# A hybrid decoder layer on one core: modulation rows by feature block, scaled rows on ScalarE, a down projection in four column passes

## The chip, the core and the metric

The kernel runs on one core of a Trainium2 chip. Each core has a TensorE for matmuls, VectorE and ScalarE for elementwise work, GpSimd, and SyncE (SP), whose queue issues all transfers of this kernel. The metric is device time in microseconds for one execution; lower is better.

## The reference

One residual layer with two sub-layers, on 256 tokens of 2048 features. A conditioning vector c gives six rows of 2048 numbers: shift, scale and gate for either sub-layer.

```
mod = silu(c) @ w_mod + b_mod                  # 2048 x 12288
sh1, sc1, g1, sh2, sc2, g2 = split(mod, 6)
u = x * (1 + sc1) + sh1
y = token_mixer(u, ...)                        # input projection, mLSTM and HGRN2 heads, w_out
x = layer_norm(ALPHA * x + (1 + g1) * y) * ln1_g + ln1_b
u = x * (1 + sc2) + sh2
y = (silu(u @ w_gate) * (u @ w_up)) @ w_down   # 2048 -> 5632 -> 2048
out = layer_norm(ALPHA * x + (1 + g2) * y) * ln2_g + ln2_b
```

## The kernel before

All weights are float32 and are read once, 512 KB at a time. A weight tile is split into a rounded high part (a copy on ScalarE) and the rest (a subtraction on VectorE); the activations are split in the same way, and every product is three matmuls: high x high, low x high, high x low (`three`, lines 709 to 716). `w1` (line 698 on) issues one tile's transfer on SP's queue into one of 4 raw buffers (`wr`) and makes the two halves, of which 5 each are kept (`wh`, `wl`). The splits have a raised priority.

A modulation row block is 128 output features of `mod`: `mod(j)` (lines 171 to 175) reads 1 MB of transposed `w_mod` into one of two buffers (`mr`) and reduces it on VectorE against silu(c) into column j of `modc`. There are 96: 0 to 15 shift 1, 16 to 31 scale 1, 32 to 47 gate 1, 48 to 63 shift 2, 64 to 79 scale 2, 80 to 95 gate 2. The first 32 belong to the head. Sections 2 and 4 are spread over the rest of the input projection and the output projection: `mods_some(RATE[...])` adds a rate per weight step and takes a row whenever a whole one has come together; `run(modq)` (line 775) takes what is left.

The output projection (lines 749 to 774) runs in four 512-column blocks c, with two PSUM banks for the two token blocks t, its residual (`resid`) and statistics (`stat`) behind each. Then follows the transition to the FFN. Line 776 makes `Ac` = ln1_g x scale and folds ln1_b x scale into the initial value of the rows 48 to 63 (line 778), so that these rows come out as the full bias of u. The rows 48 to 55 (`EARLY`) are taken next. `norm1(t)` normalizes the four blocks of z[t] in place. `make_u2(t, c)` transposes four 128 x 128 blocks of z into a PSUM bank, and for each feature block k makes the scaled row twice: ScalarE writes the high part straight into `u2h`, rounded (line 807), VectorE makes it once more in full (line 809) and subtracts (line 810). For token block 0 and k from 8 on, the row 48 + k is taken inside this loop, and a manual dependence (line 804) holds it behind the first normalizing operation. Token block 1's `make_u2` is written behind all of token block 0's.

The FFN's first two groups run together over 16 steps k with 8 PSUM banks, 24 matmuls of 512 columns a step; the first two steps are done for token block 0 before block 1's rows exist (lines 861 to 874). The groups 2 to 5 follow one at a time; the rows 80 to 95 and the affine of z (lines 884, 885) are written inside them. `down(k0, k1, ...)` runs the down projection over the hidden blocks so far, twice in all (0 to 23, 24 to 43), in two passes e of 1024 columns with four banks. In the very last pass the last two steps k are done for token block 0 first (`skew`), so that its end, `finish(0)`, can overlap with the rest of block 1.

The order on each engine comes from a planner that ranks by program order and raised priority, but starts what is ready early when an engine and a buffer are free in its model. Each engine then runs its own list strictly in that order.

Of the kernel before, what the change touches and what calls it, by code (L numbers as in the profile page):

```python
# [37 lines left out]
EARLY = 8  # L38
# [16 lines left out]
RATE = (0.4, 0.3, 0.4)  # L55
# [24 lines left out]
def build(nc, tc, d):  # L80
    from contextlib import ExitStack

    with ExitStack() as ctx:
# [532 lines left out]
        modq = chain(*[mod_pe(PE_SECT.index(s), s) if s in PE_SECT else chain(*[mod(16 * s + k) for k in range(16)]) for s in (2, 4)])  # L616
# [159 lines left out]
        tt(Ac, pc("l1g", 0, 16), modc[:, 64:80], ALU.mult)  # L776
        tt(Bc, pc("l1b", 0, 16), modc[:, 64:80], ALU.mult)
        tt(init[:, 48:64], init[:, 48:64], Bc, ALU.add)
# [5 lines left out]

        for k in range(EARLY):
            run(mod(48 + k))

        def norm1(t):
            mu, rs = norm(t)
            for c in range(4):  # L790
                w = slice(512 * c, 512 * c + 512)
                i = ts(z[t][:, w], z[t][:, w], mu, rs, ALU.subtract, ALU.mult).ins
                if t == 0 and c == 0:
                    table["first"] = i

        def make_u2(t, c):
            bank = ps()
            for j in range(4):
                nc.tensor.transpose(bank[:, P * j : P * j + P], z[t][:, 512 * c + P * j : 512 * c + P * j + P], ident)
            for j in range(4):  # L800
                k = 4 * c + j
                if t == 0 and k >= EARLY:
                    run(mod(48 + k))
                    tc.add_manual_dep(table["mod"], table["first"].name, order, reason="norm")
                o = bank[:, P * j : P * j + P]
                h = u2(u2h, k, t)
                act(h, o, AF.Identity, scale=Ac[:, k : k + 1], bias=col(3, k))
                u = S(P, "t", bufs=CFG["t"])
                ts(u, o, Ac[:, k : k + 1], col(3, k), ALU.mult, ALU.add)  # L809
                tt(u2(u2l, k, t), u, h.bitcast(F32), ALU.subtract)  # L810
# [44 lines left out]
        use = False  # L855
        for c in range(4):
            make_u2(0, c)
# [8 lines left out]
        for c in range(4):  # L866
            make_u2(1, c)
        for k in range(2):
            block(k, 1)
        for k in range(2, KT):  # L870
            for g in range(2):
                held[k, g] = w1(d["wf"][g * KT + k])
            for t in range(2):
                block(k, t)
        pend = []
# [32 lines left out]
        def down(k0, k1, G, last):  # L908
            for e in range(2):
                bk = [[ps(), ps()] for t in range(2)]  # L910
                held = {}
                skew = 2 if last and e else 0
                for k in range(k0, k1):
                    held[k] = w1(d["wd"][44 * e + k])
# [96 lines left out]
```

## Time and profile before

| | us |
|---|---|
| median of 3 runs | 1316.38 |
| lowest and highest | 1313.13, 1317.86 |
| profiled execution, whole time | 1315.63 |
| its span, first to last instruction | 1313.8 |
| TensorE, VectorE, ScalarE busy | 1222.5, 913.0, 585.3 |

The span is one execution of the kernel under the profiler. A busy share over the whole span mixes stages with different limits; the slices and the windows show where an engine falls short. "Idle before" names what ended an engine's wait.

### The profile page before, as it was taken

How to read it: one execution, taken by the hardware profiler on the slowest of the kernel's cores; microseconds unless marked ns; L12 is line 12 of the kernel's file. 1: busy time of each engine (PE TensorE's matmuls, PEld its weight loads, DVE VectorE, ACT ScalarE, POOL GpSimd, SP SyncE). 2: the span in 40 equal slices, each digit the busy share in tenths (PEclk: the TensorE clock that was granted, in tenths of full speed). 3: DMA queues.
4: the chain of work that ended last, by engine and by line, in shares of the span. 5: the costliest groups of instructions: out<-in, count | busy, mean ns of one | idle time of the engine just before them, and what ended most of it. 6: DMA issues, size and time to landing. Idle time of an engine off the chain costs nothing.

```text
span 1313.8 us, 17232 instructions
## 1 busy us (share of the span) xinstructions
PE 1222.5 (93%) x6738; PEld 1048.4 (80%) x6738; DVE 913.0 (69%) x1026; ACT 585.3 (45%) x728; POOL 3.9 (0%) x13
## 2 busy tenths in 40 slices
PE   4899999899999996289999999999999999999994
PEld 4889999898989885168888888888888888888883
DVE  6789997999998799997845444445455444445555
ACT  4563445545656433234444444433334444434330
POOL 0000000000000000000000000000000000000000
PEclk9999999899999998689999999999999999999997
DMA  9999997667988889689856566566666666676651
GB/s 368 370 339 349 352 404 259 241 225 248 323 304 327 337 325 350 240 307 331 293 189 191 184 196 186 170 193 194 194 192 192 191 184 188 193 253 191 192 162 65
DMA packets 75970, 328.03 MB, mean 250 GB/s; under 512 B 8432, under 2 KB 8816, under 8 KB 62704
## 3 DMA queue, kind: packets, MB, share of 16 engines
q1 hardware_dynamic: 75888, 326.92, 72.0%
q8 instruction: 53, 0.87, 0.3%
q14 instruction: 29, 0.24, 0.0%
HBM read 324.79 MB, written 2.10 MB: 249 GB/s over the span
## 4 chain that ended last, share of the span: by engine, by line
PE 86%; DVE 8%; DMA 2%; issue 2%; ACT 1%; DVEq 0%; SPq 0%; ACTq 0%
PE ps L716 20%; PE ps L713 20%; PE ps L712 20%; PE ps L249 5%; PE ps L251 5%; PE ps L250 5%; DVE m L174 4%; DMA m<-in_wmod 2%; PE ps L260 2%; PE ps L261 2%; PE ps L262 2%; PE ps L445 1%; DVE wl L213 1%; PE ps L835 1%; DVE wl L706 1%
## 5 line engine op out<-in xcount | busy, mean ns | idle before, releaser
L128 ACT ACTIVATE wh<-wr 128x1024 fp32r<-128x1024 f32 x408 | 431.1, 1059 | 569.7 <-PE ps L713 426.9
L706 DVE TENSOR_TENSOR wl<-wr,wh 128x1024 fp32r<-128x1024 f32 x296 | 361.5, 1225 | 327.5 <-ACT wh L128 326.9
L712 PE MATMUL ps<-wh,u2h 128*128 128x512 f32 x704 | 277.2, 394 | 10.1 <-DVE t L809 9.8
L713 PE MATMUL ps<-wh,u2l 128*128 128x512 f32 x704 | 276.0, 393 | 2.0 <-DVE u2l L810 2.0
L174 DVE CUSTOM_DVE_ANT_0 m<-m,cb,init 128x2048 f32<-128x2048 f32 x96 | 225.1, 2346 | 10.5 <-DMA m<-in_wmod 10.1
L716 PE MATMUL ps<-wl,u2h 128*128 128x512 f32 x704 | 220.4, 393 | 2.5 <-DVE wl L706 2.4
L249 PE MATMUL ps<-uh,wh 128*128 128x256 f32 x640 | 185.1, 294 | 22.3 <-ACT wh L128 16.7
L250 PE MATMUL ps<-ul,wh 128*128 128x256 f32 x640 | 181.6, 286 | 0.0
L251 PE MATMUL ps<-uh,wl 128*128 128x256 f32 x640 | 180.3, 287 | 1.1 <-DVE wl L213 1.0
L712 PEld LDWEIGHTS ps<-wh,u2h 128*128 128x128 f32 x704 | 133.6, 190 | 39.0 <-DVE t L809 10.7
L716 PEld LDWEIGHTS ps<-wl,u2h 128*128 128x128 f32 x704 | 133.3, 190 | 31.3 <-DVE wl L706 3.3
L713 PEld LDWEIGHTS ps<-wh,u2l 128*128 128x128 f32 x704 | 133.6, 190 | 30.1 <-DVE u2l L810 2.4
L213 DVE TENSOR_TENSOR wl<-wr,wh 128x1024 fp32r<-128x1024 f32 x112 | 135.8, 1221 | 27.0 <-ACT wh L128 26.4
L249 PEld LDWEIGHTS ps<-uh,wh 128*128 128x128 f32 x640 | 124.2, 196 | 24.9 <-ACT wh L128 17.1
L712 PE MATMUL ps<-wh,hid 128*128 128x512 f32 x352 | 137.2, 390 | 0.0
L713 PE MATMUL ps<-wh,hid 128*128 128x512 f32 x352 | 137.0, 389 | 0.0
L250 PEld LDWEIGHTS ps<-ul,wh 128*128 128x128 f32 x640 | 124.7, 195 | 1.2 <-issue 1.0
L251 PEld LDWEIGHTS ps<-uh,wl 128*128 128x128 f32 x640 | 123.2, 194 | 1.9 <-DVE wl L213 1.8
L716 PE MATMUL ps<-wl,hid 128*128 128x512 f32 x352 | 108.4, 389 | 0.0
L713 PEld LDWEIGHTS ps<-wh,hid 128*128 128x128 f32 x352 | 66.1, 188 | 13.7
L716 PEld LDWEIGHTS ps<-wl,hid 128*128 128x128 f32 x352 | 66.1, 188 | 13.7
L712 PEld LDWEIGHTS ps<-wh,hid 128*128 128x128 f32 x352 | 66.1, 188 | 13.6
(177 smaller groups left out, 1031.2 us busy)
## 6 DMA issues: line engine op xcount, KB each, us to landing
m<-in_wmod SPq DMA_DIRECT2D x96, 1024.0 KB, 6.5
wr<-in_wf SPq DMA_DIRECT2D x176, 512.0 KB, 3.6
wr<-in_win SPq DMA_DIRECT2D x112, 512.0 KB, 5.9
wr<-in_wd SPq DMA_DIRECT2D x88, 512.0 KB, 3.6
wr<-in_wo SPq DMA_DIRECT2D x32, 512.0 KB, 5.0
xT<-in_x SPq DMA_DIRECT2D x4, 512.0 KB, 7.7
z<-in_xr SPq DMA_DIRECT2D x2, 1024.0 KB, 7.3
out<-z SPq DMA_DIRECT2D x8, 256.0 KB, 2.4
```

The lines of the kernel that those rows point to most:

```text
L128: i = nc.scalar.activation(out, in_, f, **kw).ins
L174: table["mod"] = nc.vector.tensor_tensor_reduce(t, t, cb, 1.0, init[:, j : j + 1], ALU.mult, ALU.add, modc[:, j : j + 1]).ins
L213: tt(l[:, :m], r[:, :m], h[:, :m].bitcast(F32), ALU.subtract)
L249: mm(o, h[:, wsl], kt(uh, k0 + k), start=st, stop=False, skip_group_check=True)
L250: mm(o, h[:, wsl], kt(ul, k0 + k), start=False, stop=False, skip_group_check=True)
L251: mm(o, l[:, wsl], kt(uh, k0 + k), start=False, stop=en, skip_group_check=True)
L260: mm(o, a, h[:, w], start=first and k == 0, stop=False, skip_group_check=True)
L261: mm(o, a, l[:, w], start=False, stop=False, skip_group_check=True)
L706: tt(l, r, h.bitcast(F32), ALU.subtract)
L712: mm(o, a, h[:, w], start=first, stop=False, skip_group_check=True)
L713: mm(o, b, h[:, w], start=False, stop=False, skip_group_check=True)
L716: mm(o, a, l[:, w], start=False, stop=last, skip_group_check=True)
```

## The change

Sections 3 and 4 (shift 2, scale 2) are ordered by feature block: after the 16 gate rows come the pairs 64 + k, 48 + k. The first 34 rows of this list are spread by raised rates up to the end of the output projection; the other 14, for k = 9 to 15, are taken two at a time in the k loop of the FFN's first two groups from k = 2 on. `Ac` and `Bc` are made per 512-column block c (`affine1`), with Bc = ln1_b x scale + shift as a column of its own. The scaled rows of c = 0 and 1 are made at once for both token blocks, those of c = 2 and 3 at k = 4 and k = 8; their transposes are copied from PSUM into two tiles `zt` by ScalarE meanwhile. A scaled row is made once, by ScalarE, in full; the high part is a copy of four rows at once on ScalarE and the low part one subtraction on VectorE. The manual dependence is gone. The down projection runs in four passes of 512 columns with two banks, a weight tile holding two steps k of 512 columns; the skew of the last pass is 8 steps k.

```diff
--- before.py
+++ after.py
@@ -35,7 +35,7 @@
 
 STAGES = stages(("fq qk g i v", 4), ("qk g i v", 8), ("fq qk g i v", 16), ("o", 16))
 LAG = 0
-EARLY = 8
+FIRST = 34
 MIX = (("qk g i", "first"), ("v", "second"), ("o", "p last n"))
 NATIVE = ((), ())
 PRI = dict(w=400, e=0, m=-200)
@@ -52,7 +52,7 @@
 
 PE_SECT = ()
 DVE_SECT = ()
-RATE = (0.4, 0.3, 0.4)
+RATE = (0.45, 0.4, 0.5)
 CFG = dict(big=10, med=10, wr=4, mr=2, wh=5, wl=5, s5=4, t=3, cm=2)
 
 
@@ -613,7 +613,8 @@
         from itertools import chain
 
         gt["x"] = 0
-        modq = chain(*[mod_pe(PE_SECT.index(s), s) if s in PE_SECT else chain(*[mod(16 * s + k) for k in range(16)]) for s in (2, 4)])
+        order2 = list(range(32, 48)) + [j + k for k in range(KT) for j in (64, 48)]
+        modq = (None for j in order2[:FIRST] for _ in mod(j))
         credit = [0.0]
 
         def mods_some(a):
@@ -773,41 +774,60 @@
                         resid(t, c, banks[c][t], G1, ALPHA)
                         stat(t, c)
         run(modq)
-        tt(Ac, pc("l1g", 0, 16), modc[:, 64:80], ALU.mult)
-        tt(Bc, pc("l1b", 0, 16), modc[:, 64:80], ALU.mult)
-        tt(init[:, 48:64], init[:, 48:64], Bc, ALU.add)
+        late = order2[FIRST:]
+
+        def some(n):
+            for _ in range(n):
+                if late:
+                    run(mod(late.pop(0)))
+
+        def affine1(c):
+            w = slice(4 * c, 4 * c + 4)
+            tt(Ac[:, w], pc("l1g", 4 * c, 4), modc[:, 64 + 4 * c : 68 + 4 * c], ALU.mult)
+            tt(Bc[:, w], pc("l1b", 4 * c, 4), modc[:, 64 + 4 * c : 68 + 4 * c], ALU.mult)
+            tt(Bc[:, w], Bc[:, w], modc[:, 48 + 4 * c : 52 + 4 * c], ALU.add)
+
+        affine1(0)
+        affine1(1)
         u2h = [M(name="u2h", dt=F32R) for _ in range(4)]
         u2l = [M(name="u2l", dt=F32R) for _ in range(4)]
 
         def u2(tiles, k, t):
             return tiles[k // 4][:, (k % 4) * T + t * P : (k % 4) * T + t * P + P]
-
-        for k in range(EARLY):
-            run(mod(48 + k))
 
         def norm1(t):
             mu, rs = norm(t)
             for c in range(4):
                 w = slice(512 * c, 512 * c + 512)
-                i = ts(z[t][:, w], z[t][:, w], mu, rs, ALU.subtract, ALU.mult).ins
-                if t == 0 and c == 0:
-                    table["first"] = i
-
-        def make_u2(t, c):
+                ts(z[t][:, w], z[t][:, w], mu, rs, ALU.subtract, ALU.mult)
+
+        zt = {}
+
+        def turn(t, c):
             bank = ps()
             for j in range(4):
                 nc.tensor.transpose(bank[:, P * j : P * j + P], z[t][:, 512 * c + P * j : 512 * c + P * j + P], ident)
+            if c < 2:
+                zt[t, c] = bank
+                return
+            if t == 0:
+                zt[c] = M(name="zt")
+            zt[t, c] = zt[c][:, 512 * t : 512 * t + 512]
+            act(zt[t, c], bank, AF.Copy)
+
+        def make_u2(t, c):
+            u = S(512, "s5", bufs=CFG["s5"])
             for j in range(4):
                 k = 4 * c + j
-                if t == 0 and k >= EARLY:
-                    run(mod(48 + k))
-                    tc.add_manual_dep(table["mod"], table["first"].name, order, reason="norm")
-                o = bank[:, P * j : P * j + P]
-                h = u2(u2h, k, t)
-                act(h, o, AF.Identity, scale=Ac[:, k : k + 1], bias=col(3, k))
-                u = S(P, "t", bufs=CFG["t"])
-                ts(u, o, Ac[:, k : k + 1], col(3, k), ALU.mult, ALU.add)
-                tt(u2(u2l, k, t), u, h.bitcast(F32), ALU.subtract)
+                w = slice(P * j, P * j + P)
+                act(u[:, w], zt[t, c][:, w], AF.Identity, scale=Ac[:, k : k + 1], bias=Bc[:, k : k + 1])
+
+            def part(x):
+                return x[c].rearrange("p (k t) -> p k t", t=T)[:, :, t * P : t * P + P]
+
+            u3 = u.rearrange("p (k t) -> p k t", t=P)
+            act(part(u2h), u3, AF.Copy)
+            tt(part(u2l), u3, part(u2h).bitcast(F32), ALU.subtract)
 
 
         NG = DFF // 512
@@ -852,9 +872,10 @@
             return bk, held, block
 
         norm1(0)
-        use = False
         for c in range(4):
-            make_u2(0, c)
+            turn(0, c)
+            if c < 2:
+                make_u2(0, c)
         norm1(1)
         use_set(AF.Silu)
         tc.add_manual_dep(table["load"], table["var"].name, order, reason="table")
@@ -864,7 +885,9 @@
                 held[k, g] = w1(d["wf"][g * KT + k])
             block(k, 0)
         for c in range(4):
-            make_u2(1, c)
+            turn(1, c)
+            if c < 2:
+                make_u2(1, c)
         for k in range(2):
             block(k, 1)
         for k in range(2, KT):
@@ -872,6 +895,13 @@
                 held[k, g] = w1(d["wf"][g * KT + k])
             for t in range(2):
                 block(k, t)
+            some(2)
+            for c in (2, 3):
+                if k == 4 * c - 4:
+                    some(max(0, len(late) - 8 * (3 - c)))
+                    affine1(c)
+                    make_u2(0, c)
+                    make_u2(1, c)
         pend = []
         for g in range(2):
             for t in range(2):
@@ -906,27 +936,32 @@
                 pend.append(g)
 
         def down(k0, k1, G, last):
-            for e in range(2):
-                bk = [[ps(), ps()] for t in range(2)]
+            for c in range(4):
+                bk = [ps(), ps()]
                 held = {}
-                skew = 2 if last and e else 0
-                for k in range(k0, k1):
-                    held[k] = w1(d["wd"][44 * e + k])
+                skew = 8 if last and c == 3 else 0
+
+                def pair(k, t):
+                    for j in range(2):
+                        w = slice(512 * j, 512 * j + 512)
+                        three([bk[t]], held[k][0][:, w], held[k][1][:, w], hslice(k + j, t, 0), hslice(k + j, t, 1), k + j == k0, k + j == k1 - 1)
+
+                for k in range(k0, k1, 2):
+                    held[k] = w1(d["wd"][22 * c + k // 2])
                     if k < k1 - skew:
                         for t in range(2):
-                            three(bk[t], *held[k], hslice(k, t, 0), hslice(k, t, 1), k == k0, k == k1 - 1)
-                    if k == k0 + 2:
+                            pair(k, t)
+                    if k == k0 + 4:
                         while pend:
                             flip(pend.pop(0))
                 for t in range(2):
-                    for k in range(k1 - skew, k1):
-                        three(bk[t], *held[k], hslice(k, t, 0), hslice(k, t, 1), False, k == k1 - 1)
-                    for i in range(2):
-                        resid(t, 2 * e + i, bk[t][i], G, None)
-                        if last:
-                            stat(t, 2 * e + i)
-                    if last and e:
-                        finish(t)
+                    for k in range(k1 - skew, k1, 2):
+                        pair(k, t)
+                    resid(t, c, bk[t], G, None)
+                    if last:
+                        stat(t, c)
+                        if c == 3:
+                            finish(t)
 
         def finish(t):
             mu, rs = norm(t)
@@ -973,7 +1008,7 @@
     a["wg"] = tile(np.concatenate([wi[:, 3072:3076], z, wi[:, 3076:3080]], axis=1), 0, KT, 0, 36)
     a["wo"] = np.stack([tile(wo, 8 * part + 2 * p, 2, 512 * i, 512) for part in (1, 0) for i in range(4) for p in range(4)])
     a["wf"] = np.stack([np.concatenate([tile(wg, k, 1, 512 * g, 512), tile(wu, k, 1, 512 * g, 512)], axis=1) for g in range(DFF // 512) for k in range(KT)])
-    a["wd"] = np.stack([tile(wd, k, 1, 1024 * e, 1024) for e in range(2) for k in range(FB)])
+    a["wd"] = np.stack([tile(wd, k, 2, 512 * c, 512) for c in range(4) for k in range(0, FB, 2)])
     a["xr"] = x[0].reshape(2, P, D)
     for n, v in (("l1g", ln1_g), ("l1b", ln1_b), ("l2g", ln2_g), ("l2b", ln2_b)):
         a[n] = v.reshape(1, D)
```

## Rows read from the trace of the kernel before

**Rows 1.** The page: busy time of TensorE with its share of the span, and its busy tenths in 40 equal slices of the span (32.8 us each).

```profile
PE 1222.5 (93%) x6738; PEld 1048.4 (80%) x6738; DVE 913.0 (69%) x1026; ACT 585.3 (45%) x728; POOL 3.9 (0%) x13
...
PE   4899999899999996289999999999999999999994
```

**Rows 2.** Busy time by stretch. Columns: the stretch in us and its length; PE, PEld, DVE, ACT and POOL busy us with the number of instructions; mean granted TensorE clock; DMA share; GB/s.

```profile
164.00:197.00 33.00, 33.00 (x278) 33.00 (x277) 30.39 (x28) 16.29 (x20) 0.00 (x0) 1.00 1.01 405
230.00:263.00 33.00, 28.45 (x352) 27.50 (x353) 32.41 (x45) 19.44 (x32) 0.00 (x0) 0.90 0.68 240
430.00:506.00 76.00, 76.00 (x337) 62.74 (x335) 65.38 (x72) 32.06 (x34) 0.00 (x0) 1.00 0.89 332
506.00:586.00 80.00, 37.72 (x136) 28.84 (x136) 78.27 (x132) 22.26 (x43) 0.00 (x0) 0.70 0.79 289
586.00:645.00 59.00, 59.00 (x261) 48.84 (x261) 47.17 (x45) 26.16 (x25) 0.00 (x0) 1.00 0.90 331
```

**Rows 3.** The waits between 506 and 586 us: engine, line, whom it waited for, us in total, times, longest.

```profile
PE ps L799 <- DVE t L809: 18.1, 2, 13.7
ACT u2h L128 <- DVE modc L174: 10.7, 4, 3.7
...
PE ps L712 <- DVE t L809: 9.8, 2, 6.1
```

**Rows 4.** Groups of VectorE between 506 and 586 us: line, engine, operation, out<-in, shapes, count; busy us, mean ns of one; idle before.

```profile
L174 DVE CUSTOM_DVE_ANT_0 m<-m,cb,init 128x2048 f32<-128x2048 f32 x17 | 39.9, 2345 | 1.2 <-DMA m<-in_wmod 1.2
L809 DVE TENSOR_SCALAR t<-ps,sc,modc 128x128 f32<-128x128 f32 x32 | 12.4, 404 | 0.0
L706 DVE TENSOR_TENSOR wl<-wr,wh 128x1024 fp32r<-128x1024 f32 x8 | 9.5, 1220 | 0.0
L810 DVE TENSOR_TENSOR u2l<-t,u2h 128x128 fp32r<-128x128 f32 x31 | 8.3, 283 | 0.0
L884 DVE SCALAR_TENSOR_TENSOR z<-z,bc 128x512 f32<-128x512 f32 x6 | 4.1, 682 | 0.0
...
L792 DVE TENSOR_SCALAR z<-z,mv 128x512 f32<-128x512 f32 x8 | 4.1, 540 | 0.5 <-ACT mv L128 0.5
```

**Rows 5.** VectorE in order of time, the modulation: start us, us, engine, line, operation, out<-in, shapes, count.

```profile
440.28 0.17 DVE L776 TENSOR_TENSOR sc<-pk,modc 128x16 f32<-128x16 f32 x1
...
502.20 2.34 DVE L174 CUSTOM_DVE_ANT_0 m<-m,cb,init 128x2048 f32<-128x2048 f32 x1
...
511.41 2.34 DVE L174 CUSTOM_DVE_ANT_0 m<-m,cb,init 128x2048 f32<-128x2048 f32 x1
...
546.92 2.34 DVE L174 CUSTOM_DVE_ANT_0 m<-m,cb,init 128x2048 f32<-128x2048 f32 x1
...
551.05 2.35 DVE L174 CUSTOM_DVE_ANT_0 m<-m,cb,init 128x2048 f32<-128x2048 f32 x1
```

**Rows 6.** TensorE in order of time around the hole: start us, us, engine, line, operation, out<-in, shapes, count, and in brackets the idle time before with what ended it.

```profile
505.11 0.39 PE L716 MATMUL ps<-wl,yh 128*128 128x512 f32 x1
...
505.79 0.39 PE L716 MATMUL ps<-wl,yh 128*128 128x512 f32 x1
515.77 3.68 PE L799 MATMUL ps<-kc,z 128*128 128x128 f32 x16 [9.59 <-DVE z L792]
519.10 1.43 PE L712 MATMUL ps<-wh,u2h 128*128 128x512 f32 x4
...
585.74 0.96 PE L716 MATMUL ps<-wl,u2h 128*128 128x512 f32 x3 [2.45 <-DVE wl L706]
```

**Rows 7.** Groups of TensorE between 506.1 and 585.7 us, the matmuls of the FFN (columns as in rows 4).

```profile
L712 PE MATMUL ps<-wh,u2h 128*128 128x512 f32 x35 | 16.1, 473 | 10.1 <-DVE t L809 9.8 <-ACT wh L128 0.3
L713 PE MATMUL ps<-wh,u2l 128*128 128x512 f32 x35 | 15.6, 457 | 2.0 <-DVE u2l L810 2.0
L716 PE MATMUL ps<-wl,u2h 128*128 128x512 f32 x32 | 12.9, 469 | 0.0
```

**Rows 8.** Groups of the whole span by form: VectorE's subtraction over 512 columns (line 231), ScalarE's scaled row and its rounding copy of 512 columns; and a pair of scaled rows on ScalarE in order of time.

```profile
L128 ACT ACTIVATE u2h<-ps,modc,sc 128x128 fp32r<-128x128 f32 x32 | 14.2, 456 | 38.7 <-DVE t L809 22.6 <-DVE modc L174 10.7 <-PE ps L799 5.4
...
L231 DVE TENSOR_TENSOR hid<-ps,hid 128x512 fp32r<-128x512 f32 x22 | 14.0, 682 | 0.0
...
L128 ACT ACTIVATE hid<-ps 128x512 fp32r<-128x512 f32 x22 | 11.6, 586 | 0.0
...
519.72 0.81 ACT L128 ACTIVATE u2h<-ps,modc,sc 128x128 fp32r<-128x128 f32 x2 [2.33 <-DVE t L809]
```

**Rows 9.** VectorE in order of time, the last weight splits ahead of the norm.

```profile
504.47 4.63 DVE L706 TENSOR_TENSOR wl<-wr,wh 128x1024 fp32r<-128x1024 f32 x4
```

**Rows 10.** The end in order of time: VectorE's first residual of the last block, the last matmuls, VectorE's last scaling.

```profile
1291.85 1.29 DVE L723 TENSOR_TENSOR s<-ps,bc 128x512 f32<-128x512 f32 x2 [8.79 <-PE ps L716]
...
1294.14 0.61 PE L716 MATMUL ps<-wl,hid 128*128 128x512 f32 x2
...
1308.85 1.41 DVE L936 SCALAR_TENSOR_TENSOR z<-z,mv,bc 128x512 f32<-128x512 f32 x2
```

**Rows 11.** Transfers of the modulation rows: issues from 586 to 660 us with KB each and median us to landing; the queue of SP in order of time; the reductions between 586 and 645 us.

```profile
m<-in_wmod SPq DMA_DIRECT2D x6, 1024.0 KB, 7.9
...
519.38 49.00 SPq L173 DMA_DIRECT2D m<-in_wmod  x13
...
L174 DVE CUSTOM_DVE_ANT_0 m<-m,cb,init 128x2048 f32<-128x2048 f32 x8 | 18.8, 2350 | 6.1 <-DMA m<-in_wmod 6.1
```

## The prediction, made blind

> **What bounds the kernel now.** First the page's busy shares and its 40 slices [rows 1]: TensorE is busy 93% of the span, and only three places fall short of nines: the first two slices, slices 16 to 18, and the last one. The head isn't touched by the change, so the middle and the end are what it can move. Then the windows [rows 2]: from 430 to 506 us and from 586 to 645 us TensorE is busy throughout; from 506 to 586 it is busy 37.7 of 80 us, at a mean granted clock of 0.70, while VectorE is busy 78.3 of the 80 and ScalarE 22.3. VectorE is therefore the bound of that hole. The waits of TensorE there [rows 3] name it too: the transposes of line 799 wait 18.1 us for line 809, the scaled row made on VectorE, and matmuls wait 9.8 us for the same line. ScalarE waits 10.7 us for columns of the modulation (modc).
>
> What VectorE does there [rows 4]: 17 modulation reductions of 2.35 us, 39.9 us in all; 32 pairs of lines 809 and 810, 20.7 us; the rest is weight splitting, the affine and the norm. The order in time [rows 5] explains the hole. Program order makes all of token block 0's scaled rows, which need every shift row 48 to 63, before any of block 1's, and the k loop needs both blocks. The reductions from 511.41 to 546.92 us are these rows; those from 551.05 on are rows of section 5, which run ahead of their place while block 1's scaled rows wait their turn. That running ahead is seen elsewhere as well: the scales' product (line 776), written behind the whole output projection, ran at 440.28 us. So the rates in RATE set a floor to the pace of the rows, not the pace itself.
>
> How large the loss is: the last matmul of the output projection starts at 505.79 us, steady work begins at 585.74 us [rows 6]. Three matmuls take 0.68 us (505.11 to 505.79), 0.227 each, and 102 FFN matmuls were done in between [rows 7], worth 23.1 us. The stretch from 506.0 to 585.7 us, 79.7 us, thus loses 56.6 us.
>
> **The change part by part.**
> *The transition.* The first pair of FFN groups has 16 steps of 24 matmuls, 384 x 0.227 = 87.1 us. Before, 282 of them were left at 585.7 us, so the pair ends at 585.7 + 64.0 = 649.7 us. After the change:
> - Feature blocks 0 and 1 (k = 0 to 7) of both token blocks need only rows 64 to 71 and 48 to 55, all within the first 34. The 14 rows left over no longer stand before any matmul of k = 0 to 7, which are 8 x 5.44 = 43.5 us of TensorE work.
> - The norm's chain stays. I keep 506.0 to 519.1 us [rows 6] for the gap. Now four scaled rows are finished together: ScalarE's four at 0.36 to 0.46 us [rows 8], a rounding copy of 512 columns and a VectorE subtraction of 512 columns, at 0.59 and 0.68 us by the nearest forms [rows 8]. From the first transposes at 515.77 us that is about 0.6 for a first four at the low clock, then 1.6 + 0.6 + 0.7, some 519.7 us for the first complete operands. Before, the matmuls started at 519.1 and waited 2 us more for the low half.
> - After that gap the matmuls run at the lower of the two clock levels for a while: the windows from 506 us average 0.70 [rows 2]. Until about 526 us at half speed, 6.3 us of time, costs 3.2 us. Block 1's 16 transposes, (519.1 - 515.8) / 16 = 0.21 us each at the low clock and half of that at the full one, cost 1.7 us inside the stream.
> - VectorE is relieved: per four rows it had 4 x (0.404 + 0.283) = 2.75 us [rows 4] and now has 0.68, over 8 fours 22.0 down to 5.5 us. ScalarE, idle in 58 of the 80 us [rows 2], takes up 8 copies and 4 copies of transposes, 7 us: hidden. The nine small products of affine1 come to under 2 us; they are hidden in the same way, and would cost that much if VectorE is full.
>
> Undisturbed, the pair ends at 519.7 + 87.1 + 3.2 + 1.7 = 611.7 us, 38.0 us earlier.
>
> *What is late next.* c = 2 needs 6 of the 14 rows at about 519.7 + 4.9 + 43.5 = 568 us, c = 3 needs all at about 590 us. VectorE's work from 509 us, when the last four splits before the norm end [rows 9], to 590 us: 14 rows at 2.35 = 32.9; 19 weight splits at 1.22 = 23.2; the norm's scaling 8 x 0.54 = 4.3; subtractions 5.5; residuals and statistics left over, five operations of about 0.68 and two aggregations, 3.9; a dozen affines at 0.68 = 8.2 [rows 4]. That is 78.0 of 81 us, 96%. The nearest row for such a load is the stretch from 230 to 263 us [rows 2], VectorE 32.4 of 33 us and TensorE idle for 4.55 us of it. Two and a half such stretches would lose 11 us; with the splits given priority over the rows nothing need be lost. I take 8 us, bounds 0 and 28 (the transfers, below). Bytes: 14 rows of 1.05 MB, 17 weight tiles of 0.52 MB and a broadcast of 1.05 MB are 24.6 MB in 82 us, 300 GB/s, under the 332 GB/s at which 430 to 506 us ran with TensorE full [rows 2]. The transition gains 38.0 - 8 = 30.0 us.
>
> *The queues that the rows are moved past.* SP issues rows and weight tiles in one order, and a row waits there for one of two buffers; behind it wait the weight tiles of the next steps, then ScalarE's copies, VectorE's splits and TensorE. On ScalarE the scaled rows of c = 2 and 3 wait for modc, with weight copies queued behind them. Both are priced as rivals.
>
> *Rows earlier.* From 0.4, 0.3, 0.4 to 0.45, 0.4, 0.5 a row: the largest effect is where VectorE is full, about 24 steps x 0.05 = 1.2 rows of 2.35 us in the stretch that begins at 230 us. Cost between 0 and 2.8 us; I take 1, as TensorE falls short in only one window there. By 506 us 71 of the 96 reductions had started, the last at 502.20 [rows 5]; less the 32 of sections 0 and 1 that is 39, so asking for 34 is no extra load in sum.
>
> *Down projection.* The matmuls are the same in number, size and weight loads, the tiles the same 512 KB: nothing. Its end [rows 10]: VectorE works without a break from 1291.85 to 1310.26 us, 15.5 us past TensorE's last matmul (1294.14 + 0.61). It holds the residuals of two column blocks for both token blocks, 12 operations at 0.6, then the final scaling. After the change the residuals of c = 2 run beside the last pass, 6 x 0.6 = 3.6 us less; the skew of 8 instead of 2 double-width steps lets block 0 end 24 instead of 12 matmuls before block 1, 2.7 us sooner; against that the two short waits for the variance on ScalarE have less to fill them, 0.5 to 1.3 us. Gain 5.0 to 5.8, I take 5.3 us. The last transfer behind it stays.
>
> **Sum.** 30.0 - 1 + 5.3 = 34.3 us off the profiled execution's 1315.6 us is 1281.3 us; against the median of 1316.4 us, 1282.1 us. The profiled run lies 0.75 us under the median, which is less than any bound here. I predict 1282 us.
>
> One rule of the skill speaks against a part of this. The Trainium skill, ScalarE: Activation LUTs, section Rules for kernel authors, says to do multiplications and additions on VectorE and not on ScalarE. Here a 128-column scaling takes 0.456 us on ScalarE against 0.404 on VectorE [rows 4, 8], so the rule holds for one operation; but VectorE is the full engine of the hole and ScalarE the empty one, and by the rule alone the change would have to lose 8 x 4 x 0.05 = 1.7 us where the sum sees a gain of 16.5 us of VectorE time.
>
> **The rivals.**
> *The transfers set the pace.* If all 14 rows are still to come when the k loop reaches k = 2, each of the seven steps from 2 to 8 asks for two rows and two tiles, 3.15 MB. At 332 GB/s that is 9.5 us against 5.44 of matmuls: 28 us lost in place of 8, so 1302 us. For it: the issue order in the text is just that. Against it: rows run ahead, and four or five fit into the gap before 519 us.
> The Trainium skill, Perfetto Trace Analysis, section Roofline, gives about 435 GB/s as the ceiling of a single core; at that rate a step would take 7.2 us and the loss would be 13 us. The best stretch here, 164 to 197 us, moved 405 GB/s [rows 2].
>
> *Rows done early, the norm's way free.* If nearly all rows run ahead and the two reductions at 502.20 and 511.41 us no longer stand before the last statistics, there is no stall and the gap shrinks by two rows: 8 + 4.7 us more, 1269 us.
>
> *The hole moves.* Stalls eat the whole transition and only the end gains: 1310 us or so. For that the seven steps would have to take 5.44 + 38 / 7 = 10.9 us each.
>
> *In lockstep, slower.* The row's issue waits for a reduction, the reduction stands behind splits, these wait for buffers that TensorE frees, and the next weights stand behind the row on SP. Then a step is a chain: 5.44 of matmuls, 7.9 us for a row to land [rows 11] and two reductions, 18 us. Seven steps lose 88 us, less 38 and 4.3: 1316 + 46 = 1362 us. It turns slower from a step of about 11.5 us on. Against it: beside the FFN from 586 to 645 us, eight reductions passed the same queues and TensorE missed nothing [rows 2], and from 519 us 13 rows were issued in 49 us [rows 11], 3.8 us each.
> The Trainium skill, TensorE: Matmul & The Clock Gate, section Part 1, calls ScalarE and VectorE strict FIFOs; that is what such a lockstep needs, and the order in time of the rows above is in keeping with it.
>
> **How the numbers follow.** Forecast with stalls of 0 to 16 us (1274 to 1290): 0.60. Transfers (1290 to 1304): 0.20. Early rows (1267 to 1274): 0.10. The hole moves (1304 to 1316): 0.06. Lockstep: 0.04. The range takes in the forecast, the early rows and most of the transfers: 1268 to 1302 us. About 0.5% or 6.6 us is what a measurement of this kernel can tell from no change; below 1309.8 us lie the first three and part of the fourth: faster 0.92, same 0.04, slower 0.04.
>
> **What would show it.** Right: TensorE idle some 13 us from 506 us and then busy with few gaps; lines 809 and 810 gone from VectorE; reductions of rows 57 to 79 between the splits of k = 2 to 8; VectorE's end some 10 us after the last matmul. Wrong: TensorE waiting at k = 5 to 8 for weight tiles, or at k = 8 and 12 for scaled rows, the norm later than 514 us, or a new gap in the stretch that begins at 230 us.

## The result, and the profile after

| | before | after |
|---|---|---|
| median, us | 1317.12 (1313.13 to 1318.16, 4 runs) | 1268.04 (1264.93 to 1270.38, 4 runs) |
| profiled execution, us | 1315.63 | 1270.38 |
| its span, us | 1313.8 | 1268.6 |

The ratio is 0.9631, 95% interval 0.9602 to 0.9661: 49 us between the medians, 45.2 us between the two profiled executions. The forecast was 1282 us; the measured time is that of its rival "rows done early, the norm's way free" (1269). It lies 0.04 us above the lower end of the stated range (1268 to 1302) and outside the stretch that had most of the chance (1274 to 1290). One of five further executions of the unaltered change took 1682.1 us at a mean granted clock of 0.685; the ratios leave it out.

The page, against [rows 1]. In place of the three weak slices in the middle there is one 8:

```profile
PE 1216.6 (96%) x6738; PEld 1045.5 (82%) x6738; DVE 900.4 (71%) x979; ACT 588.6 (46%) x740; POOL 3.9 (0%) x13
...
PE   4899999899999999899999999999999999999995
```

Busy time by stretch, against [rows 2] (columns as there; the stretch from 506 us is cut in two). From 520 to 645 us TensorE misses nothing; before, it was busy for 33.3 of the 66 us from 520 to 586. The stretch that begins at 230 us is as it was:

```profile
230.00:263.00 33.00, 28.56 (x351) 27.48 (x350) 32.20 (x47) 19.78 (x32) 0.00 (x0) 0.90 0.65 231
...
506.00:520.00 14.00, 7.68 (x33) 6.41 (x32) 14.00 (x22) 7.00 (x15) 0.00 (x0) 0.80 0.99 389
520.00:586.00 66.00, 66.00 (x295) 54.02 (x294) 59.55 (x69) 39.60 (x62) 0.00 (x0) 0.99 0.84 302
586.00:645.00 59.00, 59.00 (x270) 49.09 (x269) 50.34 (x49) 27.10 (x30) 0.00 (x0) 1.00 0.93 340
```

VectorE's groups between 506 and 586 us, against [rows 4]. The two lines of scaled rows are gone, 5.5 us of subtractions are left, and 24 weight splits stand where there were 8:

```profile
L707 DVE TENSOR_TENSOR wl<-wr,wh 128x1024 fp32r<-128x1024 f32 x24 | 28.4, 1218 | 2.0 <-ACT wh L128 2.0
L174 DVE CUSTOM_DVE_ANT_0 m<-m,cb,init 128x2048 f32<-128x2048 f32 x11 | 25.7, 2345 | 3.6 <-DMA m<-in_wmod 3.6
L830 DVE TENSOR_TENSOR u2l<-s,u2h 128x512 fp32r<-128x512 f32 x8 | 5.5, 686 | 0.9 <-ACT u2h L128 0.9
```

VectorE in order of time: three modulation reductions, the lines between them left out. The one at 505.23 is the 72nd of 96 (71 start before 499 us). Less the 32 of the head that is 40 done before the norm, where the text asked for 34. Of the rows of shift 2 and scale 2 all for c = 0, 1 and 2 are then there; the eight for c = 3 follow from 517.31 to 563.52:

```profile
505.23 2.34 DVE L174 CUSTOM_DVE_ANT_0 m<-m,cb,init 128x2048 f32<-128x2048 f32 x1
...
517.31 2.34 DVE L174 CUSTOM_DVE_ANT_0 m<-m,cb,init 128x2048 f32<-128x2048 f32 x1
...
563.52 2.34 DVE L174 CUSTOM_DVE_ANT_0 m<-m,cb,init 128x2048 f32<-128x2048 f32 x1
```

TensorE in order of time, against [rows 6]. The wait before the transposes fell from 9.59 to 6.32 us, but the output projection ended 3.4 us later in this execution, so that the transposes start where they did. In four more profiles of kernels with the same program up to there (the unaltered change again, the scaled rows on both engines, the old down projection, the skew of 2) the projection's last matmul starts between 505.50 and 507.71 us and the wait is 6.31 to 6.36 us. The shorter wait thus belongs to the change; the later end varies from profile to profile, and its cause is not shown. The first four matmuls take 2.00 us, the lower clock level, the next pairs 0.62:

```profile
509.19 0.39 PE L717 MATMUL ps<-wl,yh 128*128 128x512 f32 x1
515.89 3.67 PE L809 MATMUL ps<-kc,z 128*128 128x128 f32 x16 [6.32 <-DVE z L802]
519.47 2.00 PE L713 MATMUL ps<-wh,u2h 128*128 128x512 f32 x4
521.30 0.62 PE L714 MATMUL ps<-wh,u2l 128*128 128x512 f32 x2
```

The end, against [rows 10]: token block 0's last residual, TensorE's last matmul, VectorE's last operation. From the end of the one (1254.86) to the end of the other (1265.11) it is 10.2 us, before 15.5:

```profile
1249.46 0.69 DVE L724 TENSOR_TENSOR s<-ps,bc 128x512 f32<-128x512 f32 x1 [6.07 <-PE ps L717]
...
1254.47 0.39 PE L717 MATMUL ps<-wl,hid 128*128 128x512 f32 x1
...
1263.70 1.41 DVE L971 SCALAR_TENSOR_TENSOR z<-z,mv,bc 128x512 f32<-128x512 f32 x2
```

The last Silu products of the first pair of FFN groups, first before, then after, start 39.9 us earlier:

```profile
652.15 1.28 DVE L825 TENSOR_TENSOR s<-s,ps 128x512 f32<-128x512 f32 x2
612.27 1.28 DVE L845 TENSOR_TENSOR s<-s,ps 128x512 f32<-128x512 f32 x2
```

With 5.3 us at the end this is the whole difference of the spans. Everything was gained at the two places that the prediction named, and nothing in between; the 3.4 us by which the projection ended later are already taken off.

### The profile page after: what moved, and what is told of

It is laid out like the page before. It is cut to its first block, busy times and chain, and to the rows that moved or that the text cites. A ratio compares the mean times of both kernels' runs of the same rounds, so it can differ in the third digit from the quotient of the medians.

```text
span 1268.6 us, 17191 instructions
## 1 busy us (share of the span) xinstructions
PE 1216.6 (96%) x6738; PEld 1045.5 (82%) x6738; DVE 900.4 (71%) x979; ACT 588.6 (46%) x740; POOL 3.9 (0%) x13
## 4 chain that ended last, share of the span: by engine, by line
PE 89%; DVE 6%; ACT 2%; issue 2%; DMA 1%; DVEq 0%; ACTq 0%
PE ps L713 21%; PE ps L714 21%; PE ps L717 21%; PE ps L249 5%; PE ps L251 5%; PE ps L250 5%; DVE m L174 2%; PE ps L260 2%; PE ps L261 2%; PE ps L262 2%; PE ps L445 1%; DVE wl L213 1%; ACT wh L128 1%; PE ps L855 1%; DMA m<-in_wmod 1%
## 5 line engine op out<-in xcount | busy, mean ns | idle before, releaser
L717 PE MATMUL ps<-wl,u2h 128*128 128x512 f32 x704 | 217.2, 389 | 0.0
L717 PE MATMUL ps<-wl,hid 128*128 128x512 f32 x352 | 137.0, 389 | 0.0
L714 PEld LDWEIGHTS ps<-wh,hid 128*128 128x128 f32 x352 | 66.1, 188 | 13.5
```

What stands on the lines that cost most here:

```text
L714: mm(o, b, h[:, w], start=False, stop=False, skip_group_check=True)
L717: mm(o, a, l[:, w], start=False, stop=last, skip_group_check=True)
```

## The experiments

The theory to begin with: the order by feature block makes the gain in the middle, VectorE's relief comes second, the end gives some 5 us. The rival: VectorE's relief makes it, in whatever order. The expectations name their own theories A and B, run by run.

**The scaled rows on both engines again, in the new order.** The edit, with the lines of the loop left out:

```diff
-                act(u[:, w], zt[t, c][:, w], AF.Identity, scale=..., bias=...)
-            act(part(u2h), u3, AF.Copy)
-            tt(part(u2l), u3, part(u2h).bitcast(F32), ALU.subtract)
+                act(h, o, AF.Identity, scale=..., bias=...)
+                ts(u, o, Ac[:, k : k + 1], Bc[:, k : k + 1], ALU.mult, ALU.add)
+                tt(u2(u2l, k, t), u, h.bitcast(F32), ALU.subtract)
```

> The changed kernel, but each scaled row made twice again, rounded on ScalarE and in full on VectorE with a subtraction for each 128 columns; the new order of rows stays. Theory A (what closed the hole is the order: the scaled rows of feature blocks 0 and 1 no longer stand behind the last shift rows): VectorE gets 16 us more work but the reductions were done some 20 us before they were needed, so at most a few us: 1268 to 1274. Theory B (what closed it is the relief of VectorE, which was busy 78 of 80 us): the 16.5 us are back on the path, 1280 to 1286.

Measured 1277.21 us, ratio 0.9707 (0.9688 to 0.9726): 9 us of the gain are lost, a fifth. Windows of this kernel (columns as above): VectorE is full from 520 to 540 us, and TensorE misses 3.8 us there, 1.1 us in the next window and 1.9 us from 600 to 620 us, 6.8 us of the 9:

```profile
520.00:540.00 20.00, 16.22 (x72) 11.55 (x71) 20.00 (x33) 11.41 (x24) 0.00 (x0) 1.00 0.74 273
540.00:560.00 20.00, 18.88 (x81) 14.68 (x80) 17.75 (x36) 7.14 (x9) 0.00 (x0) 1.00 0.93 336
...
600.00:620.00 20.00, 18.08 (x78) 14.29 (x78) 17.94 (x20) 9.48 (x11) 0.00 (x0) 1.00 0.92 319
```

In the new order VectorE's relief is worth 9 us. The rule quoted in the prediction from the Trainium skill (ScalarE: Activation LUTs, Rules for kernel authors: multiplications and additions belong on VectorE) gives the wrong sign here for the move as a whole, which also turns 32 subtractions of 128 columns into 8 of 512.

**The old order, the scaled rows on ScalarE.**

```diff
-order2 = list(range(32, 48)) + [j + k for k in range(KT) for j in (64, 48)]
+order2 = list(range(32, 48)) + list(range(64, 80)) + list(range(48, 64))
```

together with the old places of `make_u2` and of the shift rows, and the manual dependence. These go together; no run takes them apart.

> The changed kernel, but with the old order of modulation rows and of scaled rows: sections 2 and 4 first, then the rows 48 to 63, all four blocks c of token block 0 before those of token block 1, the rows from 56 on held behind the first normalization; the scaled rows stay on ScalarE. Theory A: the hole is back, less the work taken from VectorE: 1268 + 38 - 14, some 1292 (1284 to 1302). Theory B: nearly nothing is lost, 1268 to 1276.

Measured 1296.16 us, 0.9852 (0.9833 to 0.9871): the order is worth 28 us. Waits from 506 to 600 us (us in total, times, longest). Besides 6.6 us for the norm, one wait of TensorE stands out, for ScalarE's rows, and ScalarE waits for the bias columns of the later blocks (sc, line 788), which are made from the shift rows:

```profile
PE ps L713 <- ACT u2h L128: 22.7, 1, 22.7
...
ACT s L128 <- DVE sc L788: 16.1, 2, 14.0
```

**The old rates.** `RATE` is 0.4, 0.3, 0.4 again.

> The changed kernel with the old rates 0.4, 0.3, 0.4 and still 34 rows before the transition. In the changed kernel the output projection ends 3.4 us later than before, yet the normalization starts at the same 515.2 us, since VectorE's list sets it. Theory A (hidden there): TensorE ends the projection about 3 us earlier and then waits 3 us longer: 1266 to 1270, no measurable difference. Theory B (the higher rates cost TensorE time that is lost for good): 3.4 us faster, 1264 to 1265.

Measured 1270.74 us, 0.9661 (0.9643 to 0.968). The output projection ends 2.7 us earlier than in the second profile of the unaltered change (its last matmul at 505.03 and 507.71 us), but hardly earlier than in two other profiles with the new rates (505.50 and 505.65), so that this is not shown to come from the rates. The wait for the norm is 1.8 us longer (8.13 and 6.31), and the time is 2 us above the unaltered change, with intervals that just overlap. The higher rates cost nothing that can be measured.

**The old down projection.** `down` with two passes of 1024 columns and the skew of 2, and its weight layout.

> The changed kernel with the old down projection: two passes of 1024 columns, the last two steps skewed. Theory A: only the end changes, VectorE's work behind the last matmul goes from 10.3 back to 15.5 us: 5.2 us slower, 1273. Theory B (the four passes also change the stream of matmuls or the weights' buffers): another number, and TensorE's busy windows before the end differ.

Measured 1273.4 us, 0.9682 (0.966 to 0.9705), 5 us slower; 15.5 us from the end of the last matmul (1250.67) to VectorE's end (1266.17):

```profile
1250.05 0.62 PE L717 MATMUL ps<-wl,hid 128*128 128x512 f32 x2
...
1264.76 1.41 DVE L966 SCALAR_TENSOR_TENSOR z<-z,mv,bc 128x512 f32<-128x512 f32 x2
```

**The change unaltered, once more.** It ran in one set with the next three kernels.

> The changed kernel once more, unaltered. Its first profile ended the output projection 3.4 us later than the kernel before, while two kernels with the same program up to there (the old down projection, the scaled rows on both engines) did not. Theory A (a stall of that one execution): the projection ends at about 506 us and the transposes start at about 512.4 us; median 1265 to 1268. Theory B (a cost of the higher rates): 509 us again.

Measured 1268.62 us, 0.9628 (0.9612 to 0.9645). The projection's last matmul starts at 507.71 us and the transposes at 514.41, between the two theories: neither a stall of a single execution nor a fixed cost of the rates is shown.

**All 14 late rows held behind the norm.** The edit, without the lines that remember the first normalizing operation:

```diff
                     run(mod(late.pop(0)))
+                    tc.add_manual_dep(table["mod"], table["first"].name, order, reason="norm")
```

> The changed kernel with the 14 late modulation rows held behind the first normalizing operation; in the changed kernel 6 of them ran ahead of it. Theory A (the gap before the FFN is VectorE's list: what stands ahead of the norm there delays it): the reduction that ran at 505.23 us is gone from it and the four splits stand partly behind, 2 to 4 us faster, 1262 to 1265, as the 24 us by which the rows were early pay for the later start. Theory B (the late rows had no reserve): TensorE waits at k = 8 and 12, 1270 or more.

Measured 1278.85 us, 0.9712 (0.9694 to 0.9729): 10 us slower, though TensorE waits only 2.7 us in all for the normalized blocks. SP's queue in order of time (start, us until the last of the group was issued, count): two rows, one weight tile, two rows, one weight tile, 9 us a turn. The rows' issues wait for buffers that reductions free, and the tiles stand behind them:

```profile
548.28 3.80 SPq L173 DMA_DIRECT2D m<-in_wmod  x2
552.17 0.38 SPq L702 DMA_DIRECT2D wr<-in_wf  x1
557.60 3.20 SPq L173 DMA_DIRECT2D m<-in_wmod  x2
560.90 0.38 SPq L702 DMA_DIRECT2D wr<-in_wf  x1
566.55 3.80 SPq L173 DMA_DIRECT2D m<-in_wmod  x2
```

The waits from 540 to 580 us: ScalarE waits 29.1 us for weight tiles, and TensorE 7.8 us for ScalarE. The third line is from SP's own waits from 495 to 590 us, the rows' issues waiting for reductions:

```profile
ACT wh L128 <- DMA wr<-in_wf: 29.1, 8, 8.0
...
PE ps L713 <- ACT wh L128: 7.8, 2, 5.1
...
SPq L173 <- DVE modc L174: 45.1, 12, 6.0
```

This has the queue of the prediction's rival "the transfers set the pace", but not its price. A turn of 9 us holds two rows and one tile, where the rival gave two rows and two tiles 9.5 us, and 10 us are lost in all, where it gave 28. The issue that waits for a reduction is the link of the lockstep rival, at half its step of 18 us. Whether the bytes (301 GB/s from 548.28 to 566.55 us) or that chain sets the 9 us, no run separates. With the head start of six rows, none of it showed.

**The norm's chain first.** Raised priority for the residuals and statistics of the output projection's last block and for `norm1(0)`.

```diff
+                        with tc.high_priority(1000 if c == 3 else 0):
                             resid(t, c, banks[c][t], G1, ALPHA)
                             stat(t, c)
...
+        with tc.high_priority(1000):
             norm1(0)
```

> The changed kernel with a raised priority for the last block's residuals and statistics of the output projection and for the first normalization, above that of the weight splits. Theory A (VectorE's list sets the gap): two of the four splits stand behind the norm, 2.3 us faster, 1264 to 1266. Theory B (the chain from the last matmul through the variance sets it): no change, 1266 to 1269.

Measured 1265.19 us, 0.9608 (0.9591 to 0.9625), 3.4 us under the unaltered change, with intervals that overlap a little. In order of time (columns as before, all engines): one reduction still stands before token block 0's last statistics, the aggregate comes at 508.36 us in place of 514.44, and the wait is 3.31 us in place of 6.32:

```profile
503.16 2.35 DVE L174 CUSTOM_DVE_ANT_0 m<-m,cb,init 128x2048 f32<-128x2048 f32 x1
...
508.36 0.25 DVE L735 BATCH_NORM_AGGREGATE mv<-st 128x2 f32<-128x24 f32 x1
...
510.80 3.60 PE L810 MATMUL ps<-kc,z 128*128 128x128 f32 x16 [3.31 <-DVE z L803]
```

**Both together.** The hold of all 14 rows and the raised priority.

> Both edits: late rows held behind the first normalization, and the raised priority of the last residuals and the norm. Theory A: the idle time ahead of the first transposes falls from 6.3 us to 2 us or less; 4 to 5 us faster than the changed kernel, 1262 to 1264. Theory B: as the changed kernel or slower.

Measured 1277.77 us, 0.97 (0.9685 to 0.9715): TensorE waits 0.8 us in all for the normalized blocks, but then misses 3.6 us from 540 to 560 and 4.6 us from 560 to 580.

**Four passes, but a skew of 2.** `skew = 2 if last and c == 3 else 0`.

> The changed kernel with its four passes, but a skew of 2 steps k in the last one in place of 8. Block 0 of tokens then ends 6 matmuls ahead of block 1 (1.4 us) in place of 24 (5.4 us). Theory A (the lead of block 0 is what gains at the end, the width of the pass a little): VectorE ends some 13.8 us behind the last matmul in place of 10.3, 3.5 us slower than the changed kernel, 1270 to 1272. Theory B (the narrow pass alone gains): 1267 to 1269.

Measured 1271.88 us, 0.9648 (0.9632 to 0.9664). The interval overlaps that of the unaltered change (0.9612 to 0.9645), so the trace has to tell. From the end of the last matmul (1253.13) to VectorE's end (1266.67) it is 13.5 us:

```profile
1252.74 0.39 PE L717 MATMUL ps<-wl,hid 128*128 128x512 f32 x1
...
1265.26 1.41 DVE L971 SCALAR_TENSOR_TENSOR z<-z,mv,bc 128x512 f32<-128x512 f32 x2
```

The passes with the short skew thus give 2.0 of the 5.3 us at the end, the longer skew 3.3.

**The old order, and the rows on both engines.** The edits of the first two experiments together.

> The changed kernel with both halves of the transition undone: the old order of rows and scaled rows made on both engines; the copies of the transposes for c = 2 and 3, the new rates and the new down projection stay. Undone alone, the order cost 28 us and the relief 9 us. Theory A (they add up, nothing else in the transition matters): about 1268 + 37 + some 3 where both hit the same chain, 1305 to 1311. Theory B (the PSUM copies close part of the hole by themselves): under 1303.

Measured 1296.16 us, 0.9836 (0.9819 to 0.9853): as with the rows on ScalarE. In the old order, with the copies in place, VectorE's relief is worth nothing, and yet this run stands 21 us under the kernel before, of which the end explains 5.

**The same without the copies to `zt`.**

```diff
-            if c < 2:
-                zt[t, c] = bank
-                return
-            if t == 0:
-                zt[c] = M(name="zt")
-            zt[t, c] = zt[c][:, 512 * t : 512 * t + 512]
-            act(zt[t, c], bank, AF.Copy)
+            zt[t, c] = bank
```

> The old order with the rows made on both engines, as in e10_order_vec, and the transposes of the blocks c = 2 and 3 left in their PSUM banks again, with no copy to zt. Of the old kernel's middle only the rates and the affine by blocks are then changed; the end is the new one. Theory A: what kept e10 some 16 us under the old kernel, beyond the end's 5, were the copies, since a bank that waits for its rows holds up the next block's transposes and with them block 1's scaled rows: 1309 to 1313 us, and the transposes of block 1 wait for VectorE's scaled rows (line 809 of the kernel before) until about 550 us again. Theory B: the copies have no part in it (it is the affine in small pieces, or the rates): 1294 to 1299 us.

Measured 1314.22 us, 0.9972 (0.9962 to 0.9982). The four copies are worth 18 us in the old order. TensorE's waits from 506 to 600 us, first with the copies:

```profile
PE ps L714 <- DVE u2l L829: 15.1, 2, 14.0
...
PE ps L812 <- DVE z L803: 12.6, 3, 6.5
...
PE ps L812 <- DVE t L828: 0.5, 1, 0.5
```

and without them:

```profile
PE ps L812 <- DVE t L822: 23.6, 3, 17.2
PE ps L713 <- DVE t L822: 9.8, 2, 6.1
...
PE ps L812 <- DVE z L803: 7.1, 1, 7.1
```

Without them block 1's transposes (L812) wait 23.6 us for scaled rows: a bank is free only when VectorE has read its block 0 rows, and these need shift rows. With the copies that wait is 0.5 us, though TensorE then waits 15.1 us for the low halves of the rows themselves and 5.5 us more for normalized blocks.

**A further step: the norm first, and only the last 9 rows held.** This takes the one reduction out of the norm's way and puts off one row instead of six. To the edit of the norm's chain first it adds:

```diff
                     run(mod(late.pop(0)))
+                    if len(late) < 9:
+                        tc.add_manual_dep(table["mod"], table["first"].name, order, reason="norm")
```

> e7_normfirst, and the last 9 of the 14 rows may start only behind the first normalizing operation: on VectorE's list this takes out the one reduction that stood between token block 0's last residual and its statistics (503.16 us, 2.35 us). Theory A: the transposes come some 2 us earlier (508 to 509 us, idle time before them about 1.3 in place of 3.31), nothing waits in the k loop, since only one row is put off and they had some 20 us in hand: 1261 to 1264 us. Theory B: what is put off there is missing later, as it was when all 14 were held (1278): waits at k = 8 or 12, 1266 us or more. Theory C: a weight split takes the row's place and the gap stays: 1264 to 1266 us.

Measured 1264.49 us, 0.96 (0.9585 to 0.9615). VectorE in order of time: the reduction is gone, but a split comes before the aggregate and two behind it, where VectorE would wait for ScalarE's square root:

```profile
504.39 0.70 DVE L731 BATCH_NORM_STATS2 st<-z 128x6 f32<-128x512 f32 x1
505.00 1.21 DVE L707 TENSOR_TENSOR wl<-wr,wh 128x1024 fp32r<-128x1024 f32 x1
506.12 0.26 DVE L735 BATCH_NORM_AGGREGATE mv<-st 128x2 f32<-128x24 f32 x1
506.30 2.29 DVE L707 TENSOR_TENSOR wl<-wr,wh 128x1024 fp32r<-128x1024 f32 x2
...
509.11 0.54 DVE L805 TENSOR_SCALAR z<-z,mv 128x512 f32<-128x512 f32 x1
```

TensorE's waits for the normalized blocks fell from 3.3 to 2.8 us in all (three waits, the longest 2.07), and the time, against the norm first alone, by no more than the intervals allow. Of the three theories the third, that a split takes the row's place, explains it. It lies some 4 us under the change, the lowest of all kernels here, but the two intervals still overlap (0.9612 to 0.9615), so that it is not shown to be faster.

## Why the prediction came out as it did

*The bound.* That VectorE and the order of the rows bound the hole was half of it. The 18.1 us for which the transposes waited for line 809 [rows 3] were read as work that VectorE is too slow for. They were a PSUM bank held by rows whose shift rows had not come. In the old order the copies alone took this wait away and gained 18 us, with VectorE nearly as full (busy 91.83 of the 94 us from 506 to 600 with them, 93.42 without). The prediction priced the copies as work to hide and gave them no gain. The sum didn't suffer, since it was worked out from the hole as a whole and not by adding up edits. Put back from the new kernel, the steps are: the order 28 us (1296.16 to 1268.04), the copies 18 (1314.22 to 1296.16), VectorE's relief 0 before the order is changed; the relief in the old order without the copies was not tried. Taken out alone, the relief costs 9. The end is 5, and 1314.22 is 2 more than the kernel before less the end, about as much as the intervals of both leave open. Taken apart in another order the sizes would be others, as the two values for the relief show.

*The transition, undisturbed.* 38.0 us were worked out, 39.9 measured. The gap was kept from 506.0 to 519.1 us, and the first matmuls came at 519.47. That position was right by luck, as neither of its parts was: a reduction less stands before the norm (the wait is 3.3 us shorter), and the output projection ended 3.4 us later. One of the signs of being wrong did show: the norm's scaling began at 515.29 us, later than 514, though no later than before (515.17). The lower clock level was given until 526 us, 3.2 us; it ended with the first four matmuls, near 521.3 us, which cost about 1 us.

*What is late next: the step that failed.* Stalls of 8 us were put in; there were none. VectorE's load came out near (78.0 put in, 74.55 measured of the 81 us from 509 to 590), with fewer rows and more splits and affines in it. The count of the rows did not: it took 14 to be late, c = 2 needing 6 of them at 568 us. The text asks for 34 rows by the end of the output projection, and the planner ran 40, so that c = 2 needed none and c = 3 had its last column at about 566 us, 21 us before k = 12 (519.5 + 12 x 5.44 = 584.8, and 2 for the clock and the transposes). The prediction had the row that said so: it counted 39 reductions of these sections by 506 us in the kernel before and used it for the rates only. Carried on, it would have left 9 late rows. With all 14 made late, in the hold, the kernel lost 10 us net, not far from the 8 put in.

The price, too, was taken from a row that could not give it. The 4.55 us that TensorE missed in the kernel before from 230 to 263 us are two waits for one product in the token mixer (line 454):

```profile
PE ps L445 <- DVE q L454: 4.5, 2, 3.8
```

They are not what a full VectorE costs in general. In the kernel with the norm first VectorE is busy for all 20 us from 540 to 560, and TensorE misses nothing:

```profile
540.00:560.00 20.00, 20.00 (x90) 16.57 (x89) 20.00 (x22) 7.69 (x9) 0.00 (x0) 1.00 0.95 367
```

*The rival that came true.* 1269 us were given to "rows early, the norm's way free" at a chance of 0.10. Of its two parts the rows came early enough, though not nearly all of them; of the two reductions in the norm's way one left it, and the wait fell by 3.3 us where 4.7 were put in for two. The norm first took another 3 us off the wait, but by moving weight splits; holding the other reduction back gave nothing certain. That the time came within 1 us of 1269 is in part chance, as the profiled execution took 1270.38 us.

*The transfers.* Their condition, all rows still to come, wasn't met. In the hold, which comes near it, the queue went in turns of two rows and one tile, 9 us each, and the loss was 10 us in place of 28. That experiment also overturned a reading of the trace after: 21 us in hand did not mean that rows could be put off by 14 us of VectorE time. With six rows put off, the pace of the queue decides, at two rows in 9 us; with one, nothing is lost.

*Rates.* 1 us was put in, 0 to 2.8 as bounds; with the old rates the kernel is not faster, so the cost is nothing that can be measured.

*The end.* 5.3 us were put in and 5.3 measured, with the passes and the skew in about the shares given (3.6 and 2.7, less up to 1.3; measured 2.0 with half the old lead, and 3.3 for 18 matmuls of lead).

*Lockstep and the moved hole.* Neither showed: TensorE is busy throughout from 520 to 645 us.

In sum, 8 us of stalls, 1 of rates and 1.9 in the undisturbed transition make the 10.9 us between the 34.3 predicted and the 45.2 of the profiled executions. The medians lie another 3.8 us apart; the executions of the kernel after spread from 1264.93 to 1270.38 us, and the profiled one is the longest.

## What to carry to other kernels

Before charging for work that is made late, count in the trace how far the planner runs ahead of the text: the number asked for is a floor, and what is late is the rest after the number done. Before taking a loss over from a stretch where an engine is as full, look up what the idle engine waited for there. A wait for the reader of a PSUM bank is a wait for that reader's inputs too; moving the bank's content out can be worth more than making the reader faster. When a queue carries both the rows of a side job and the weights of the main one, a side job that is put off comes back as late weights, so put off as few as the gap needs.

## What the runs showed of the hardware that was not expected

The granted clock rose soon after the gap: with 6.3 us of idle time, 16 transposes in 3.67 us and four matmuls in 2.00 us before it, the next pairs ran at 0.62 us, the higher level, and the mean from 520 to 586 us was 0.99. In the kernel before, whose matmuls stopped again and again, the mean from 506 to 586 was 0.70 [rows 2]. With the rows held, SP's queue stood for 45.1 us, from 495 to 590, before rows' issues that waited for a buffer, and the weight tiles behind them stood too: rows and tiles came in turns of 9 us, and TensorE got 11.55 us of work into the 20 from 560 to 580 us, at 0.80 of the clock.
